# Low parts of weight blocks formed in one piece, and keys by three matmuls in the convolution stages

## The chip, the cores and the metric

The program runs on one core of one Trainium2 chip. The metric is the device time of one execution in microseconds (us). Engines are named as the profile names them: PE (TensorE, with PEld for its weight loads), DVE (VectorE), ACT (ScalarE), POOL (GpSimd), SP (SyncE, which issues the weight loads from memory).

## The reference

A decoder trunk of four layers works on 256 positions of width 1024, in fp32. Layers 0 and 3 mix positions with a gated causal convolution of 31 taps, layer 1 with a state-space scan, layer 2 with differential attention. Every layer then attends to 256 memory positions and ends in a gated feed-forward. Each sub-layer is added to its scaled input and normalized. What the change touches is the keys of the memory attention; every product of the kernel with a weight matrix uses the low parts.

```python
def memory_cross_attention(x, mem, w_q, w_kv, w_out):
    q = (x @ w_q).reshape(b, s, XA_HEADS, XA_HEAD_DIM) * (XA_HEAD_DIM ** -0.5)
    k, v = jnp.split(mem @ w_kv, 2, axis=-1)
    ...
    p = jax.nn.softmax(jnp.einsum('bshd,bmhd->bhsm', q, k), axis=-1)
    return jnp.einsum('bhsm,bmhd->bshd', p, v).reshape(b, s, D_MODEL) @ w_out

for i in range(DEPTH):          # 4 layers
    y = (conformer_conv, ssd_mixer, diff_attention)[i % 3](x, ...)
    x = post_norm(x, y, ...)
    x = post_norm(x, memory_cross_attention(x, mem, ...), ...)
    x = post_norm(x, swiglu(x, ...), ...)
```

## The kernel before, in words

**Products.** An fp32 product is made of matmuls in the faster type F32R. Every operand is split into a high part (rounded to that type) and a low part (what the rounding left). A product is then high by high, high by low and low by high; `mm3` writes these three matmuls (L199, L200, L201).

**Weights.** All weights pass through `_Weights` in blocks of 128 x 1024 elements, in an order that a dry run of the same program has written down (`plan`). `_load` issues a block's transfer on SP (L145) into one of four raw buffers, rounds it on ACT into the high part `wh` (L152), and subtracts on DVE for the low part `wl` (L155), in `LO_PARTS` pieces. `wh` and `wl` have seven buffers each (`RING`). A call of `get` hands out the next block and first sees to it that the three blocks after it (`AHEAD`) have been asked for.

**Memory projection.** `mem @ w_kv` does not depend on the layer's input. It is cut into eight units a layer (`kv_steps`): units 0 to 3 make 256 columns of the keys each, units 4 to 7 of the values. Units are called at fixed places, so that TensorE has work while another engine finishes a stage: in layer 0's convolution four units after the transform of the first half of the channels and three after the norm's code (`KV_CONV`), in layer 3's one and four; one after the feed-forward's first block and one after the feed-forward, for the next layer. So the convolution of layer 0 calls key units 0 to 3, and that of layer 3 key units 2 and 3.

**Keys.** A key unit runs `gemm_c_steps`. The memory's high and low parts lie side by side in one tile (`MT`, 512 columns), so one 512-column matmul (L277) multiplies the weights' high part with both; a 256-column matmul (L279) adds the low part of the weights times the high part of the memory, into the right half of the PSUM bank. Both weight blocks of the unit are asked for at the start. The two halves of 128 output columns use one bank each, out of the two of pool `psI`; `summed` evicts a half by an ACT copy of the bank's left half (L292) and a DVE add of its right half (L293), into `memK`.

**Values** use `mm3` with 256-column matmuls into a single bank of `psI`, block by block, and are split by ACT and DVE (L206, L208) into `memVh` and `memVl`.

**The convolution's tail.** After the depthwise transform, DVE and ACT normalize and gate the tile (DVE L586, L592, L595, ACT L594), TensorE transposes it (L598), and ACT and DVE split it (L206, L210) for the output product (L321, L322, L325).

**Norms.** `post_norm` is a chain of DVE steps (L365, L242, L243, L233, L372, L377) with a POOL step, then transposes (L219) and splits into `XT` (L206, L208), from which the next sub-layer starts.

**Order.** Pools, waits and the order of instructions on every engine are set when the program is built: a list scheduler with a cost model takes the next ready instruction by its place in the program, and `post_norm` is moved ahead by 400 places (`high_priority`). An engine then runs its instructions in that fixed order.

Of the kernel before, what the change touches and what calls it, by code (L numbers as in the profile page):

```python
# [60 lines left out]

RING = 7
RAW = 4
LO_PARTS = 2
AHEAD = 3
KV_CONV = ((4, 3), (1, 4))
KV_SSD = (0, 0, 0, 0, 0, 0, 0, 1, 2, 1)
# [42 lines left out]
class _Weights:  # L110
# [25 lines left out]
    def _load(self, q):  # L136
# [15 lines left out]
        nc.scalar.copy(out=wh, in_=raw)  # L152
        m = nk * n // LO_PARTS
        for a in range(0, nk * n, m):
# [9 lines left out]
class _Trunk:  # L164
# [257 lines left out]
    def kv_steps(self, layer):  # L422
        u = self.kv_next
        if u >= 8 * min(layer + 1, DEPTH):
            return
        self.kv_next += 1
        i, u = divmod(u, 8)
        nc = self.nc
        if u < 4:
            yield from self.gemm_c_steps(  # L430
                "xa_w_kv", i, ((u * 256, 256),), self.MT, self.summed(self.memK[:, 2 * u : 2 * u + 2, :])
            )
            return
        ps = self.bank("i", a=2)
        for b in range(2):
            wh, wl = self.W.get("xa_w_kv", i, 4 * b, 4, (u * 256, 256))
            for k in range(4):
                kk = 4 * b + k
                for m in range(T):
                    ms = slice(m * P, (m + 1) * P)  # L440
                    self.mm3(
                        ps[:, m, :], self.MTh[:, kk, ms], self.MTl[:, kk, ms], wh[:, k, :], wl[:, k, :],
                        kk == 0 and m == 0, kk == KT - 1 and m == 1,
                    )
            yield
        cs = slice((u - 4) * 256, (u - 3) * 256)
        self.split(ps, self.memVh[:, :, cs], self.memVl[:, :, cs])
# [911 lines left out]
    def run(self):  # L1359
        n = 0  # L1360
        ctx = ExitStack()
        pre, (loads, tables, late) = self.prepare(0, ctx, _FromRaw(self.raw))
        loads()
        self.setup()
        tables()
        pre["late"] = late
        for i in range(DEPTH):
            m, j = i % 3, i // 3
            (self.conv, self.ssd, self.diff)[m](i, j, pre)
            ctx.close()  # L1370
            if i == 0:
                self.rope()
            n += 1
            if n == self.n_sub:
                break
            self.xattn(i)
            n += 1
            if n == self.n_sub:
                break
            hooks, tmp = {}, ExitStack()  # L1380
            if i < DEPTH - 1:
                made = {}
                pre, steps = self.prepare(i + 1, ctx, _Late(made))
                made["pool"] = tmp.enter_context(self.stage_pool(f"tmp{i + 1}", 1))
                hooks = {3 + 2 * k: [step] for k, step in enumerate(steps)}
            self.ff(i, i < DEPTH - 1, hooks)
            tmp.close()
            n += 1
            if n == self.n_sub:
                break  # L1390
            self.kv_unit(i + 1)
        ctx.close()
        if n != N_SUB:
            for t in range(T):
                self.nc.sync.dma_start(out=self.out[0][t * P : (t + 1) * P, :], in_=self.x[t])
# [37 lines left out]
```

## Time and profile before

| | |
|---|---|
| median of 3 runs | 1755.23 us (1751.21 to 1758.06) |
| the profiled execution | 1751.45 us |
| its span, first to last instruction | 1749.7 us |
| PE busy, matmuls | 1705.1 us, 9692 of them |
| DVE busy | 1324.2 us, 2514 instructions |
| ACT busy | 912.6 us, 1442 instructions |
| POOL busy | 57.1 us, 72 instructions |

The profile is of one execution; times in it count from the first instruction. A matmul's record reaches beyond the start of the next one, since they are pipelined, so the rate of a stream is read from start to start. In a timeline the bracket at the end of a row gives the engine's idle time before that instruction and what ended it.

### The profile page before, as it was taken

The numbers are of one execution on the slowest core, as the hardware profiler recorded it, in microseconds if no ns is written. First come the engines' busy times: TensorE is split into PE (matmuls) and PEld (weight loads), VectorE is DVE, ScalarE is ACT, GpSimd is POOL, SyncE is SP. The second block draws the span as 40 slices with busy tenths as digits, with TensorE's granted clock in tenths as the row PEclk, the third lists the DMA queues.
The fourth block names the chain that finished last, engine by engine and source line by source line (L and its number), as shares of the span: only waits on it lengthen the run. The fifth ranks groups of instructions, "written<-read, shape, count | busy, mean of one in ns | idle before, by whom it ended". The sixth has DMA issues, their size and how long they took to land.

```text
span 1749.7 us, 26246 instructions
## 1 busy us (share of the span) xinstructions
PE 1705.1 (97%) x9692; PEld 1466.5 (84%) x9692; DVE 1324.2 (76%) x2514; ACT 912.6 (52%) x1442; POOL 57.1 (3%) x72
## 2 busy tenths in 40 slices
PE   7999999999999999999999999999999998999998
PEld 4788888888999998888888888988788787878886
DVE  5889786668998878786668677876666897876666
ACT  3545555554665655455554565645454544645552
POOL 0000000000011010000000000000000000000000
PEclk9999999999999999999999999999999999999999
DMA  7647466665755645476665543656566635646662
GB/s 232 205 126 231 137 209 188 184 190 172 222 166 171 187 145 186 121 220 190 192 192 179 183 133 109 193 167 199 171 187 191 216 109 181 192 159 193 191 190 75
DMA packets 234088, 309.86 MB, mean 177 GB/s; under 512 B 14104, under 2 KB 196774, under 8 KB 233960
## 3 DMA queue, kind: packets, MB, share of 16 engines
q1 hardware_dynamic: 233832, 307.90, 57.2%
q8 instruction: 76, 1.25, 0.3%
q14 instruction: 52, 0.43, 0.1%
q10 hardware_dynamic: 128, 0.29, 0.0%
HBM read 307.07 MB, written 1.08 MB: 176 GB/s over the span
## 4 chain that ended last, share of the span: by engine, by line
PE 81%; DVE 5%; DMA 2%; ACT 1%; issue 1%; POOL 0%; SPq 0%; DVEq 0%; ACTq 0%; POOLq 0%
PE psi L277 20%; PE psi L279 10%; PE pso L321 6%; PE pso L322 6%; PE pso L325 6%; PE psi L199 5%; PE psi L200 5%; PE psi L201 5%; PE pso L199 4%; PE pso L201 4%; PE pso L200 4%; DVE wl L155 1%; PE psm L219 1%; DVE st L242 1%; DMA raw<-in_xa_w_q 1%
## 5 line engine op out<-in xcount | busy, mean ns | idle before, releaser
L155 DVE TENSOR_TENSOR wl<-raw,wh 128x512 fp32r<-128x512 f32 x1074 | 708.2, 687 | 288.4 <-ACT wh L152 280.4
L152 ACT CAST wh<-raw 128x1024 fp32r<-128x1024 f32 x537 | 561.9, 1052 | 467.4 <-issue 125.4
L277 PE MATMUL psi<-XT,wh 128*128 128x512 f32 x1408 | 387.1, 396 | 0.0
L277 PEld LDWEIGHTS psi<-XT,wh 128*128 128x128 f32 x1408 | 243.6, 189 | 36.7 <-issue 2.4
L279 PEld LDWEIGHTS psi<-XT,wl 128*128 128x128 f32 x1408 | 216.5, 189 | 29.9
L279 PE MATMUL psi<-XT,wl 128*128 128x256 f32 x1408 | 224.4, 281 | 0.0
L321 PE MATMUL pso<-wh,ch 128*128 128x512 f32 x448 | 176.4, 394 | 0.5 <-ACT ch L206 0.5
L322 PE MATMUL pso<-wl,ch 128*128 128x512 f32 x448 | 175.4, 392 | 0.0
L325 PE MATMUL pso<-wh,cl 128*128 128x512 f32 x448 | 138.6, 391 | 0.0
L199 PE MATMUL psi<-XT,wh 128*128 128x256 f32 x384 | 111.3, 290 | 0.0
L201 PE MATMUL psi<-XT,wl 128*128 128x256 f32 x384 | 108.7, 283 | 0.0
L200 PE MATMUL psi<-XT,wh 128*128 128x256 f32 x384 | 108.6, 283 | 0.0
L325 PEld LDWEIGHTS pso<-wh,cl 128*128 128x128 f32 x448 | 84.0, 188 | 17.9
L321 PEld LDWEIGHTS pso<-wh,ch 128*128 128x128 f32 x448 | 84.1, 188 | 16.6 <-ACT ch L206 0.9
L322 PEld LDWEIGHTS pso<-wl,ch 128*128 128x128 f32 x448 | 84.2, 188 | 15.8
L199 PE MATMUL pso<-wh,XT 128*128 128x512 f32 x224 | 89.2, 399 | 0.1
L201 PE MATMUL pso<-wh,XT 128*128 128x512 f32 x224 | 88.4, 395 | 0.3 <-DVE XT L208 0.3
L200 PE MATMUL pso<-wl,XT 128*128 128x512 f32 x224 | 87.8, 392 | 0.0
L234 POOL TENSOR_TENSOR rs<-rv,mhalf 128x1 f32<-128x1 f32 (+2 forms) x40 | 37.0, 926 | 1320.8 <-DVE rv L233 1308.5
L199 PE MATMUL pso<-wh,ch 128*128 128x512 f32 x192 | 75.9, 396 | 0.0
L201 PE MATMUL pso<-wh,cl 128*128 128x512 f32 x192 | 75.1, 392 | 0.0
L199 PE MATMUL psi<-wh,MT 128*128 128x256 f32 x256 | 74.6, 291 | 0.4 <-DVE memVl L208 0.4
(324 smaller groups left out, 2941.8 us busy)
## 6 DMA issues: line engine op xcount, KB each, us to landing
raw<-in_ff_w_in SPq DMA_DIRECT2D x160, 512.0 KB, 4.6
raw<-in_ff_w_out SPq DMA_DIRECT2D x88, 512.0 KB, 4.0
raw<-in_xa_w_kv SPq DMA_DIRECT2D x64, 512.0 KB, 4.5
raw<-in_cv_w_in SPq DMA_DIRECT2D x64, 256.0 KB, 4.2
raw<-in_xa_w_q SPq DMA_DIRECT2D x32, 512.0 KB, 4.3
raw<-in_xa_w_out SPq DMA_DIRECT2D x32, 512.0 KB, 4.7
raw<-in_mb_w_in SPq DMA_DIRECT2D x32, 512.0 KB, 3.9
raw<-in_da_w_qkv SPq DMA_DIRECT2D x24, 512.0 KB, 4.6
```

Of the source, the lines that this page charges most:

```text
L152: nc.scalar.copy(out=wh, in_=raw)
L155: nc.vector.tensor_tensor(out=wl[:, a : a + m], in0=raw[:, a : a + m], in1=wh[:, a : a + m].bitcast(F32), op=ALU.subtract)
L199: mm(out, ah, bh, start=start, stop=False)
L200: mm(out, ah, bl, start=False, stop=False)
L201: mm(out, al, bh, start=False, stop=stop)
L219: nc.tensor.transpose(ps[:, i, :], nat[:, (4 * j + i) * P : (4 * j + i + 1) * P], self.ident)
L234: nc.gpsimd.tensor_tensor(out=r, in0=v, in1=self.mhalf[:, :cols], op=ALU.pow)
L277: mm(ps, wh[:, k, js], X[:, 4 * b + k, :], start=b == 0 and k == 0, stop=False)
L279: mm(ps[:, S : 2 * S], wl[:, k, js], X[:, 4 * b + k, 0:S], start=False, stop=b == 1 and k == 3)
L321: mm(acc[t][c], hh[:, ts], wh[:, 0, cs], start=first, stop=False)
L322: mm(acc[t][c], hh[:, ts], wl[:, 0, cs], start=False, stop=False)
L325: mm(acc[t][c], hl[:, ts], wh[:, 0, cs], start=False, stop=last)
```

## The change

`LO_PARTS` goes from 2 to 1: the low part of a block is one DVE instruction of 1024 columns. In the convolution stages (`in_conv`) a key unit runs `gemm_b_steps`, the form that the state-space layer uses already: three 256-column matmuls (`mm3`) for each pair of 128 rows and 128 columns, block by block, all into one PSUM bank, which a single ACT copy of 512 columns then evicts. Key units called elsewhere stay as they are.

```diff
--- before.py
+++ after.py
@@ -61,7 +61,7 @@
 
 RING = 7
 RAW = 4
-LO_PARTS = 2
+LO_PARTS = 1
 AHEAD = 3
 KV_CONV = ((4, 3), (1, 4))
 KV_SSD = (0, 0, 0, 0, 0, 0, 0, 1, 2, 1)
@@ -426,12 +426,16 @@
         self.kv_next += 1
         i, u = divmod(u, 8)
         nc = self.nc
-        if u < 4:
+        if u < 4 and not self.in_conv:
             yield from self.gemm_c_steps(
                 "xa_w_kv", i, ((u * 256, 256),), self.MT, self.summed(self.memK[:, 2 * u : 2 * u + 2, :])
             )
             return
         ps = self.bank("i", a=2)
+        if u < 4:
+            yield from self.gemm_b_steps(ps, "xa_w_kv", i, ((u * 256, 256),), self.MTh, self.MTl)
+            nc.scalar.copy(out=self.memK[:, 2 * u : 2 * u + 2, :], in_=ps)
+            return
         for b in range(2):
             wh, wl = self.W.get("xa_w_kv", i, 4 * b, 4, (u * 256, 256))
             for k in range(4):
@@ -1366,7 +1370,9 @@
         pre["late"] = late
         for i in range(DEPTH):
             m, j = i % 3, i // 3
+            self.in_conv = m == 0
             (self.conv, self.ssd, self.diff)[m](i, j, pre)
+            self.in_conv = False
             ctx.close()
             if i == 0:
                 self.rope()
```

## Rows read from the trace of the kernel before

**Rows 1.** The page: engine table, then the chain by engine and by line.
```profile
PE 1705.1 (97%) x9692; PEld 1466.5 (84%) x9692; DVE 1324.2 (76%) x2514; ACT 912.6 (52%) x1442; POOL 57.1 (3%) x72
...
PE 81%; DVE 5%; DMA 2%; ACT 1%; issue 1%; POOL 0%; SPq 0%; DVEq 0%; ACTq 0%; POOLq 0%
PE psi L277 20%; PE psi L279 10%; PE pso L321 6%; PE pso L322 6%; PE pso L325 6%; PE psi L199 5%; PE psi L200 5%; PE psi L201 5%; PE pso L199 4%; PE pso L201 4%; PE pso L200 4%; DVE wl L155 1%; PE psm L219 1%; DVE st L242 1%; DMA raw<-in_xa_w_q 1%
```

**Rows 2.** VectorE by line and form: count, busy us, mean ns, idle before.
```profile
L155 DVE TENSOR_TENSOR wl<-raw,wh 128x512 fp32r<-128x512 f32 x1074 | 708.2, 687 | 288.4 <-ACT wh L152 280.4 <-PE psm L965 1.0
...
L293 DVE TENSOR_TENSOR memK<-memK,psi 128x256 f32<-128x256 f32 x32 | 13.1, 418 | 2.0 <-ACT memK L292 1.7
...
L565 DVE SCALAR_TENSOR_TENSOR x<-x,raw 128x1024 f32<-128x1024 f32 x4 | 4.8, 1218 | 0.0
```

**Rows 3.** TensorE timeline of layer 3's convolution tail: start, us, instruction, idle before.
```profile
1436.06 0.28 PE L199 MATMUL psi<-wh,MT 128*128 128x256 f32 x1
1436.18 0.28 PE L200 MATMUL psi<-wl,MT 128*128 128x256 f32 x1
...
1443.28 0.28 PE L201 MATMUL psi<-wh,MT 128*128 128x256 f32 x1
1444.45 0.63 PE L598 MATMUL psm<-ident,cv_u 128*128 128x128 f32 x4 [0.89 <-DVE rv L233]
...
1450.00 1.09 PE L598 MATMUL psm<-ident,cv_u 128*128 128x128 f32 x4 [3.28 <-DVE cv_u L595]
1450.74 0.56 PE L199 MATMUL psi<-wh,MT 128*128 128x256 f32 x1
```

**Rows 4.** TensorE timeline of layer 0, first key unit.
```profile
61.67 0.63 PE L279 MATMUL psi<-MT,wl 128*128 128x256 f32 x4
64.99 0.43 PE L199 MATMUL psm<-ch,cv_dft0h 128*82 128x512 f32 x1 [2.69 <-DVE cvp L541]
```

**Rows 5.** VectorE timeline between the steps of a norm, layer 0.
```profile
220.25 0.68 DVE L155 TENSOR_TENSOR wl<-raw,wh 128x512 fp32r<-128x512 f32 x1
...
225.15 0.64 DVE L155 TENSOR_TENSOR wl<-raw,wh 128x512 fp32r<-128x512 f32 x1
...
228.41 1.29 DVE L155 TENSOR_TENSOR wl<-raw,wh 128x512 fp32r<-128x512 f32 x2
```

**Rows 6.** TensorE timeline in the same norm.
```profile
229.24 0.36 PE L279 MATMUL psi<-MT,wl 128*128 128x256 f32 x1
```

**Rows 7.** TensorE timeline of a key unit, layer 0.
```profile
72.01 1.08 PE L277 MATMUL psi<-MT,wh 128*128 128x512 f32 x4
72.92 0.64 PE L279 MATMUL psi<-MT,wl 128*128 128x256 f32 x4
73.40 1.09 PE L277 MATMUL psi<-MT,wh 128*128 128x512 f32 x4
```

**Rows 8.** TensorE timeline after the tail of layer 3.
```profile
1455.41 0.41 PE L201 MATMUL psi<-wh,MT 128*128 128x256 f32 x1
1455.62 0.39 PE L199 MATMUL psi<-wh,MT 128*128 128x256 f32 x1
```

**Rows 9.** ScalarE timeline in the tail of layer 3.
```profile
1436.75 0.36 ACT L292 COPY memK<-psi 128x256 f32<-128x256 f32 x1
```

**Rows 10.** VectorE timeline in the tail of layer 3.
```profile
1436.18 0.64 DVE L155 TENSOR_TENSOR wl<-raw,wh 128x512 fp32r<-128x512 f32 x1
...
1449.77 0.42 DVE L293 TENSOR_TENSOR memK<-memK,psi 128x256 f32<-128x256 f32 x1
1450.10 0.69 DVE L155 TENSOR_TENSOR wl<-raw,wh 128x512 fp32r<-128x512 f32 x1
```

**Rows 11.** Busy time by stretch: us and instructions of each engine, granted clock, DMA.
```profile
60.00:128.00 68.00, 64.87 (x380) 55.73 (x378) 57.97 (x104) 33.53 (x49) 1.11 (x2) 1.00 0.44 135
1429.00:1450.00 21.00, 16.36 (x102) 13.84 (x101) 20.06 (x39) 10.38 (x18) 1.10 (x2) 0.98 0.15 51
1449.00:1456.00 7.00, 6.00 (x29) 5.96 (x30) 7.00 (x15) 4.06 (x8) 0.00 (x0) 0.51 0.56 182
```

## Prediction

> **What bounds the kernel now.** I read the page's engine table and chain first [rows 1]: TensorE is busy for 1705.1 of 1749.7 us and holds 81% of the chain, VectorE is busy for 76% and holds 5%, with the low-part line L155 at 1%. So the matmul stream sets the time; a change that takes work off VectorE pays only where TensorE stands still for VectorE. All such standing still together is at most 1749.7 - 1705.1 = 44.6 us. Next I read VectorE by line and form [rows 2], for the size of what is edited, and then the TensorE timeline, looking for idle times in brackets; two of the larger ones lie in convolution stages: 3.28 us near 1450 and 2.69 us near 62 [rows 3, 4].
>
> **Low parts, one instruction instead of two.** There are 1074 / 2 = 537 blocks. A half of 512 columns takes 0.687 us [rows 2]; the 1024-column line L565 (other operation, same shape and element type, both tensors in SBUF) takes 1.218 us. Summed by durations a block would save 2 x 0.687 - 1.218 = 0.156 us. But VectorE's instructions overlap at their ends: 1074 x 0.687 is 738 us while the line is busy for 708.2, and two halves in a row take 1.29 us from the first's start to the second's end (last row of [rows 5]), 0.084 us less than two durations; so each frees the engine about 0.084 us before its end, a pair holds it for 1.29 - 0.084 = 1.206 us and a whole for 1.218 - 0.084 = 1.134. I take 0.07 us a block, 537 x 0.07 = 38 us of VectorE's 1324. [...]
>
> On TensorE's time this is worth 0 in my sum, because the matmuls already run over it. Bounds: if every L155 on the chain (1% of 1749.7, 17 us) shrinks by 0.07 in 1.20, -1.0 us. The other end is loss: a whole cannot be interrupted. Between the steps of a norm, VectorE now slips single halves in: four from 220.25 to 225.15 [rows 5]. If each of the four becomes a whole, the norm is 4 x 0.53 = 2.1 us later (0.53 being 1.218 - 0.687). Eleven norms feed a following sub-layer: 44 x 0.53 = 23 us. The work that hides this is the memory projection, of which pieces lie between the transposes of the norm (L279 on MT in [rows 6]); a unit holds 5.6 us of it and little is used up there. I take 0, nearer to the hidden end, since TensorE's row there has no idle time in front of it. The first use of a low part may also wait up to 0.53 us longer, but blocks are asked for three ahead, which is some 9 us of matmuls at 3.3 us a block (1749.7 / 537); in the steady stretches that stays hidden.
>
> **Keys: matmuls.** Six units change: four in layer 0, two in layer 3 (u = 2 and 3, since units 24 and 25 run in the feed-forward before). Old: per four k, four 512-column matmuls in 0.91 us and four of 256 in 0.48 [rows 7]; a unit has four such groups, 4 x 1.39 = 5.56 us. New: 48 matmuls of 256 columns, which the value units already run at 0.12 us from start to start (first two rows of [rows 3]): 5.76 us. Cost 6 x 0.20 = +1.2 us, taken in full as TensorE is the bound. [...]
>
> **Keys: eviction and bank.** A unit now has two ScalarE copies and two VectorE adds of 0.418 us [rows 2]; afterwards one ScalarE copy of 512 columns, no VectorE work. Copies: less than the two of 0.36 us that they replace [rows 9], hidden by ScalarE's idle half: 0. Adds: about 0.33 us of the engine each, 12 x 0.33 = 4 us of VectorE. What counts is which bank comes free when. In layer 3's tail ScalarE copies the second key half at 1436.75 [rows 9], but the add that frees its bank runs at 1449.77 [rows 10], behind the convolution's norm, on a VectorE that is busy for 20.06 of 21 us [rows 11]. There are two such banks and the other holds the value unit that ran from 1436.06 to 1443.28 (48 matmuls) [rows 3]. So TensorE had no bank for the next value unit: it idled 0.89 and 3.28 us and started that unit at 1450.74 [rows 3], right after the add. With the change the bank is free at about 1437.4. What is late next is the low part of that unit's weights: its halves run at 1436.18 and 1450.10 [rows 10], the first block only. As one instruction begun at 1436.18 the whole block is done at 1437.4, unless it is put behind the norm. Then TensorE has 24 matmuls x 0.12 = 2.9 us to run in the gap; the second block of 24 waits. Gain 2.9 us (bounds 0, and 4.2 for both gaps).
>
> **The clock.** [...] An idle of 2.69 us at 64.99 left the clock alone (the 60-to-128 stretch shows 1.00 [rows 11]), so with the gap broken by 2.9 us of matmuls I expect no fall: -2.5 us (bounds 0 and -2.5).
>
> **Layer 0.** At 61.67 the first key unit has run its first 4 + 4 matmuls, then TensorE waits 2.69 us for the bank of the transform [rows 4]. In the old order a unit's half needs both weight blocks; in the new one block gives 24 matmuls, 2.88 us instead of 1.39. Gain 1.5 us (bounds 0, 2.7). The second block is asked for up to 2.9 us later than now; the order of loads is the same, and three blocks ahead cover it: 0, up to 2.9 once if not.
>
> **Sum.** +1.2 - 2.9 - 2.5 - 1.5 + 0 = -5.7 us against the profiled execution's 1751.45 us (span 1749.7 and 1.75 around it): 1745.8. That execution lies 3.8 us under the median of the runs shown, 1755.23; on the median's scale I predict 1749.5, 0.3% down. About 0.5%, 8.8 us, is what a measurement of this kernel can tell from no change.
>
> **Rivals.**
> *VectorE remains the wall.* In the tail the whole low part is put behind the norm, so the free bank has nothing to run. For it: VectorE has 0.94 us of slack in 21 [rows 11], and the second half now runs only at 1450.10 [rows 10]. Against: the first half did get in at 1436.18. The tail's -5.4 is gone: +1.2 - 1.5, 1754.9.
> *More is given back.* Both tail gaps vanish (4.2), the clock holds (2.5), layer 0's gap goes entirely (2.7) and the chain's low parts shrink (1.0): +1.2 - 10.4 = -9.2, 1746.0. For it: every idle here names VectorE. Against: the second block's low part has to come from the same full engine.
> *Whole low parts hold up the norms; slower.* 0.53 us at each of 44 places [rows 5], if the projection pieces no longer cover them. It makes the kernel slower than before from 11 uncovered places on (5.7 / 0.53), slower by over 0.5% from 28 on; at 28, 1764. For it: VectorE's steps of a norm follow each other with hardly any idle. Against: no idle TensorE there now.
> [...]
>
> **Chances.** Forecast 0.43 (own range 1747 to 1753), wall 0.27, more given back 0.15, norms 0.13, loads 0.02. Faster by over 0.5%: most of the third case and the forecast's lower edge, 0.17; slower: the last two, 0.14 after some of the norm case falls short; within: 0.69. Range 1742 to 1762: it takes in the first three with some 3 us of spread between medians at either end, and leaves out the last two.
>
> **What would show it.** L155 with 537 instructions of about 1.22 us; VectorE's busy time down by some 40 us; L293 on memK 20 times instead of 32. Right: in layer 3's tail value matmuls between 1443 and 1450, no idle over 2 us there and the granted clock at 1.00. Wrong: the same 3 us of idle before L598 and the low clock behind it, or new idle of half a microsecond before XT's first matmuls at the norms. What would upset the whole is that the order written for every engine changes with 537 instructions fewer, and a new gap arises somewhere that this trace doesn't show.

## The result, and the profile after

The changed kernel takes 1745.11 us (median of 19 runs, 1740.33 to 1753.83), the kernel before beside it 1755.23 (19 runs): ratio over all runs 0.9949, 95% interval 0.9937 to 0.9960 (the two medians alone give 0.9942). That is 0.51% faster by the ratio, just over the bound that the prediction set for telling a change. 1745.1 lies in the range, 2 us under the forecast's own range and 4.4 under its 1749.5. The profiled execution took 1743.85 us, span 1742.1 against 1749.7. Line numbers shift by a few between the kernels: L602 below is L598 of the kernel before.

The page's engine table, which answers to [rows 1]:

```profile
PE 1702.5 (98%) x9788; PEld 1470.3 (84%) x9788; DVE 1283.5 (74%) x1965; ACT 907.8 (52%) x1436; POOL 67.8 (4%) x72
```

VectorE by line and form, which answers to [rows 2]:

```profile
L155 DVE TENSOR_TENSOR wl<-raw,wh 128x1024 fp32r<-128x1024 f32 x537 | 654.1, 1221 | 286.3 <-ACT wh L152 281.5 <-DMA raw<-in_xa_w_kv 1.8 <-PE psm L969 1.7
...
L293 DVE TENSOR_TENSOR memK<-memK,psi 128x256 f32<-128x256 f32 x20 | 8.2, 408 | 0.9 <-ACT memK L292 0.6
```

VectorE has 40.7 us less to do, and TensorE's busy time is 2.6 us shorter although it has 96 matmuls more. Layer 3's convolution tail, TensorE's timeline and then the windows; these answer to [rows 3, 11]:

```profile
1443.95 0.60 PE L602 MATMUL psm<-ident,cv_u 128*128 128x128 f32 x4
1444.30 0.36 PE L200 MATMUL psi<-wl,MT 128*128 128x256 f32 x1
...
1445.70 0.63 PE L602 MATMUL psm<-ident,cv_u 128*128 128x128 f32 x4
1446.08 0.36 PE L199 MATMUL psi<-wh,MT 128*128 128x256 f32 x1
```

```profile
1428.00:1449.00 21.00, 21.00 (x159) 19.85 (x158) 19.93 (x36) 11.37 (x19) 1.10 (x2) 1.00 0.32 101
```

No row there has a bracket: 0.89, 0.47 and 3.28 us of idle are gone, value matmuls run on both sides of the transposes, and the granted clock is 1.00. Layer 0's gap stayed as long, which answers to [rows 4]:

```profile
63.64 0.28 PE L201 MATMUL psi<-MT,wl 128*128 128x256 f32 x1
63.76 0.28 PE L199 MATMUL psi<-MT,wh 128*128 128x256 f32 x1
66.74 0.43 PE L199 MATMUL psm<-ch,cv_dft0h 128*82 128x512 f32 x1 [2.70 <-DVE cvp L545]
```

One place that the prediction did not look at also changed: the start of layer 3's convolution. In the kernel before, TensorE's timeline and VectorE's in the same stretch:

```profile
1364.59 1.29 PE L219 MATMUL psm<-ident,x 128*128 128x128 f32 x8
1368.59 0.47 PE L199 MATMUL psi<-wh,XT 128*128 128x512 f32 x1 [2.71 <-DVE memK L293]
```

```profile
1361.75 0.65 DVE L155 TENSOR_TENSOR wl<-raw,wh 128x512 fp32r<-128x512 f32 x1
...
1365.02 1.30 DVE L155 TENSOR_TENSOR wl<-raw,wh 128x512 fp32r<-128x512 f32 x2
1366.22 1.29 DVE L208 TENSOR_TENSOR XT<-psm,XT 128x512 fp32r<-128x512 f32 x2
1367.41 0.69 DVE L155 TENSOR_TENSOR wl<-raw,wh 128x512 fp32r<-128x512 f32 x1
1368.01 0.76 DVE L293 TENSOR_TENSOR memK<-memK,psi 128x256 f32<-128x256 f32 x2
```

Afterwards, in VectorE's timeline, the same two adds stand among the norm's steps and right behind them, both ahead of the last low part and of the second half's XT splits; TensorE is busy for all of the 12 us from 1360 on:

```profile
1361.44 0.36 DVE L293 TENSOR_TENSOR memK<-memK,psi 128x256 f32<-128x256 f32 x1
...
1364.43 0.41 DVE L293 TENSOR_TENSOR memK<-memK,psi 128x256 f32<-128x256 f32 x1
1364.76 1.22 DVE L155 TENSOR_TENSOR wl<-raw,wh 128x1024 fp32r<-128x1024 f32 x1
```

This key unit is unit 25, which runs with the old key matmuls in both kernels. So here the low parts moved the adds. That raised the question which of the two edits the gain belongs to.

### The profile page after: what moved, and what is told of

Its sections match the earlier page's. It is cut to its first block, busy times and chain, and to the rows that moved or that the text cites. A ratio compares the mean times of both kernels' runs of the same rounds, so it can differ in the third digit from the quotient of the medians.

```text
span 1742.1 us, 25792 instructions
## 1 busy us (share of the span) xinstructions
PE 1702.5 (98%) x9788; PEld 1470.3 (84%) x9788; DVE 1283.5 (74%) x1965; ACT 907.8 (52%) x1436; POOL 67.8 (4%) x72
## 5 line engine op out<-in xcount | busy, mean ns | idle before, releaser
L155 DVE TENSOR_TENSOR wl<-raw,wh 128x1024 fp32r<-128x1024 f32 x537 | 654.1, 1221 | 286.3 <-ACT wh L152 281.5
L277 PEld LDWEIGHTS psi<-XT,wh 128*128 128x128 f32 x1408 | 242.9, 189 | 37.8 <-PE psm L201 2.6
L322 PE MATMUL pso<-wl,ch 128*128 128x512 f32 x448 | 175.2, 391 | 0.0
L325 PE MATMUL pso<-wh,cl 128*128 128x512 f32 x448 | 139.8, 391 | 0.0
L234 POOL TENSOR_TENSOR rs<-rv,mhalf 128x1 f32<-128x1 f32 (+2 forms) x40 | 48.5, 1212 | 1337.0 <-DVE rv L233 1324.2
L200 PE MATMUL pso<-wl,ch 128*128 128x512 f32 x192 | 75.0, 391 | 0.0
L199 PEld LDWEIGHTS psi<-XT,wh 128*128 128x128 f32 x384 | 73.6, 192 | 0.7 <-issue 0.3
```

The costliest lines, as they stand in the source:

```text
L155: nc.vector.tensor_tensor(out=wl[:, a : a + m], in0=raw[:, a : a + m], in1=wh[:, a : a + m].bitcast(F32), op=ALU.subtract)
L199: mm(out, ah, bh, start=start, stop=False)
L200: mm(out, ah, bl, start=False, stop=False)
L234: nc.gpsimd.tensor_tensor(out=r, in0=v, in1=self.mhalf[:, :cols], op=ALU.pow)
L277: mm(ps, wh[:, k, js], X[:, 4 * b + k, :], start=b == 0 and k == 0, stop=False)
L322: mm(acc[t][c], hh[:, ts], wl[:, 0, cs], start=False, stop=False)
```

## The experiments

**Which part.** The theory of the prediction's sum, that ScalarE frees the keys' bank in time, against its rival, that whole low parts do it.

*Low parts whole, keys as before.*

```diff
-LO_PARTS = 2
+LO_PARTS = 1
```

> Whole low parts alone, key units as before. Theory of the bank (the gain of the change comes from layer 3's convolution tail, where a key half holds its bank until an add on a full VectorE): the tail keeps a gap of over 2 us before L598 and a fall of the granted clock behind it, the whole kernel changes by -2 to +2 us. Rival of the low parts (shorter VectorE work gives the gain by itself): -7 to -10 us, gap gone.

Measured: 1743.65 us beside 1752.97, ratio 0.9950 (0.9937 to 0.9962), span 1741.9. This is the whole gain without any new key unit. VectorE's busy time is 1287.2 us by the page, 37.0 under [rows 1]. Its timeline in the tail has the second half's add at 1435.60, right behind the first statistics of the convolution's norm (L581), where [rows 10] have it at 1449.77 behind the norm:

```profile
1434.89 0.67 DVE L543 TENSOR_TENSOR cv_yre<-cvp,cv_yre 81x512 f32<-81x512 f32 x1
1435.48 0.20 DVE L581 BATCH_NORM_AGGREGATE mv<-st 128x2 f32<-128x12 f32 x1
1435.60 0.36 DVE L293 TENSOR_TENSOR memK<-memK,psi 128x256 f32<-128x256 f32 x1
1435.88 0.68 DVE L544 TENSOR_TENSOR cvp<-psm,cv_H 81x512 f32<-81x512 f32 x1
```

*Keys new, low parts in halves.*

```diff
+            self.in_conv = m == 0
...
-        if u < 4:
+        if u < 4 and not self.in_conv:
...
+        if u < 4:
+            yield from self.gemm_b_steps(ps, "xa_w_kv", i, ((u * 256, 256),), self.MTh, self.MTl)
+            nc.scalar.copy(out=self.memK[:, 2 * u : 2 * u + 2, :], in_=ps)
+            return
```

> Key units of the convolution stages as in the changed kernel, low parts in two halves as before. Theory of the bank: the tail of layer 3 has a bank early, -5 to -9 us, with at most 2 us of idle left there where a second block's low part is late. Rival of the low parts: +1 us (48 matmuls for 32 in six units), gap as before. Third theory, both parts needed (the bank comes free but the low part is still behind the norm): 0 to -2 us here and in the run with whole low parts alone.

Measured: 1751.91 us, ratio 0.9996 (0.9984 to 1.0009): no change. Yet the tail's idle is gone here too. TensorE is busy for all of the tail at clock 1.00 (windows), while its timeline keeps the start's idle and shows a new one at the next norm:

```profile
1431.00:1452.00 21.00, 21.00 (x150) 19.06 (x149) 20.32 (x38) 10.91 (x17) 1.10 (x2) 1.00 0.29 94
```

```profile
1372.12 0.77 PE L199 MATMUL psi<-wh,XT 128*128 128x512 f32 x1 [2.70 <-DVE memK L293]
...
1482.45 0.39 PE L201 MATMUL pso<-wh,cl 128*128 128x512 f32 x1
1485.24 1.29 PE L219 MATMUL psm<-ident,x 128*128 128x128 f32 x8 [2.41 <-DVE x L377]
```

ScalarE's and VectorE's timelines ahead of that norm:

```profile
1477.66 1.05 ACT L152 CAST wh<-raw 128x1024 fp32r<-128x1024 f32 x1 [1.62 <-DMA raw<-in_xa_w_q]
```

```profile
1478.74 1.29 DVE L155 TENSOR_TENSOR wl<-raw,wh 128x512 fp32r<-128x512 f32 x2 [1.37 <-ACT wh L152]
1479.95 0.68 DVE L365 SCALAR_TENSOR_TENSOR x<-x,pso 128x512 f32<-128x512 f32 x1
1480.67 0.69 DVE L242 BATCH_NORM_STATS2 st<-x 128x6 f32<-128x512 f32 x1
1481.28 0.67 DVE L365 SCALAR_TENSOR_TENSOR x<-x,pso 128x512 f32<-128x512 f32 x1
```

Read from the bottom: the norm's first step L365 is written behind the low part of a block whose load came late, so that the cast waited 1.62 us for the DMA and the low part 1.37 us for the cast. TensorE, now ahead of the loads, runs out of matmuls. Part of the idle went from the tail to the norm behind it: up to that norm's first transpose this profile is 3.4 us ahead of the kernel before (129.34 against 132.75 us from the stage's first L365), and of these the medians show 1.1 (1752.97 - 1751.91), not told from nothing. Here the second L365 (1481.28) waits for nothing of TensorE's, it is only late in VectorE's order, while in the kernel before it waited 1.30 us for TensorE (VectorE's timeline):

```profile
1481.17 0.69 DVE L365 SCALAR_TENSOR_TENSOR x<-x,pso 128x512 f32<-128x512 f32 x1 [1.30 <-PE pso L201]
```

*The changed kernel, with VectorE copying the keys out.*

```diff
-            nc.scalar.copy(out=self.memK[:, 2 * u : 2 * u + 2, :], in_=ps)
+            nc.vector.tensor_copy(out=self.memK[:, 2 * u : 2 * u + 2, :], in_=ps)
```

> The changed kernel with the key units' copy out of the bank on VectorE instead of ScalarE: same matmuls, same low parts, the bank again waits for VectorE. Theory of the bank: the gap in layer 3's tail comes back, 3 us or more, and the clock falls behind it, so +5 to +8 us against the changed kernel, -4 to 0 against the kernel before. Rival of the low parts, and that of the matmul form (one bank per unit instead of one per half is what helps): within 2 us of the changed kernel, -7 to -10 against before.

Measured: 1746.35 us, ratio 0.9964 (0.9952 to 0.9977). The tail has no idle although VectorE frees the bank, at 1439.84:

```profile
1439.84 0.63 DVE L437 COPY memK<-psi 128x512 f32<-128x512 f32 x1
```

So it is not the engine that matters but the place in its order.

*The changed kernel, with new key units in layer 3 only.*

```diff
-            self.in_conv = m == 0
+            self.in_conv = i == 3
```

> The changed kernel with the new key units in layer 3's convolution alone; layer 0 keeps the old ones. Theory of the bank: the four units of layer 0 gave nothing (its gap near 62 us stayed), and cost 0.2 us each on TensorE, so -9 to -11 us against before, 0 to 1 better than the changed kernel. Rival, layer 0 has a share: -5 to -7.

Measured: 1744.06 us, ratio 0.9954 (0.9940 to 0.9968). With or without layer 0's new units the time is the same.

**Volume or order.** After these runs two theories of the whole low parts were left: VectorE has some 40 us less to do (volume), or the written order of VectorE changes so that the key adds, which free TensorE's banks, come earlier in layer 3 (order).

*Halves as before, the adds put early.*

```diff
-            self.nc.scalar.copy(out=out[:, j, :], in_=main)
-            self.nc.vector.tensor_tensor(out=out[:, j, :], in0=out[:, j, :], in1=rest, op=ALU.add)
+            with self.tc.high_priority() if early else ExitStack():
+                self.nc.scalar.copy(out=out[:, j, :], in_=main)
+                self.nc.vector.tensor_tensor(out=out[:, j, :], in0=out[:, j, :], in1=rest, op=ALU.add)
...
+                "xa_w_kv", i, ((u * 256, 256),), self.MT, self.summed(self.memK[:, 2 * u : 2 * u + 2, :], early=True)
```

> Halves as before, old keys; only the two adds of each key unit (L293 on memK) and the copies ahead of them are put into VectorE's order as early as they can run: in layer 3's tail the second half's add stands some 11 instructions earlier, at the convolution's start the two adds no longer stand behind both blocks' halves. Order theory (the gain came from adds that free a bank in time, 2.7 us at the start of layer 3's convolution, 4.2 us of gaps and 2.5 us of low clock in its tail): ratio 0.995, some 1744 to 1747 us beside a kernel before of 1753, the convolution stage of layer 3 some 118 us long instead of 126. Volume theory (40 us less VectorE work is what counts): VectorE's work is the same, so 1752 to 1754, ratio 0.9995.

Measured: 1744.7 us beside 1752.96, ratio 0.9957 (0.9941 to 0.9972), as order said. VectorE's work is unchanged (page), its timeline has the tail's second add at 1437.12, where [rows 10] have 1449.77, and TensorE is busy through the tail (windows). The edit names only the adds and the copies ahead of them; the scheduler then placed other work anew too, and in and just behind layer 3's convolution some 25 of the 198 other VectorE instructions, low parts among them, stand elsewhere in the order:

```profile
PE 1701.9 (98%) x9692; PEld 1463.8 (84%) x9692; DVE 1322.5 (76%) x2514; ACT 912.3 (52%) x1442; POOL 56.5 (3%) x72
```

```profile
1437.12 0.42 DVE L294 TENSOR_TENSOR memK<-memK,psi 128x256 f32<-128x256 f32 x1 [0.19 <-ACT memK L293]
```

```profile
1437.00:1457.00 20.00, 20.00 (x160) 19.29 (x159) 19.31 (x38) 11.85 (x22) 1.47 (x2) 1.00 0.36 122
```

*Two pieces of 960 and 64 columns.*

```diff
-        for a in range(0, nk * n, m):
+        for a, e in ((0, 960), (960, 1024)):
...
-                out=wl[:, a : a + m], in0=raw[:, a : a + m], in1=wh[:, a : a + m].bitcast(F32), op=ALU.subtract
+                out=wl[:, a:e], in0=raw[:, a:e], in1=wh[:, a:e].bitcast(F32), op=ALU.subtract
```

> A block's low part in two instructions of 960 and 64 columns instead of 512 and 512: the same number of instructions and columns, so the same VectorE time as before (some 1320 us busy), old keys. Volume theory: as before, ratio 1.000. Order theory: it depends on where the key adds fall in the written order: at the start of layer 3's convolution they stand together behind the blocks as before (2.7 us idle stays), in the tail the second add stands in the middle of the norm, some 3 us earlier than before, so that about 1 us of 4.2 idle and perhaps the clock's 2.5 us come back: ratio 0.998 to 1.000, 1749 to 1753 us. If what counts is the length of the longer piece alone: ratio 0.995.

Measured: 1757.66 us, ratio 1.0027 (1.0013 to 1.0040), outside what either theory gave. VectorE by line and form:

```profile
L154 DVE TENSOR_TENSOR wl<-raw,wh 128x960 fp32r<-128x960 f32 x537 | 620.3, 1155 | 286.7 <-ACT wh L152 274.7 <-PE psm L964 3.2 <-PE psi L276 2.6
L154 DVE TENSOR_TENSOR wl<-raw,wh 128x64 fp32r<-128x64 f32 x537 | 117.2, 218 | 0.0
```

Nearly the same VectorE time (1319.7 us by the page, 4.5 less) and a longer piece make it slower. A long piece is therefore no gain in itself. The order moved here too, and against the kernel: by the page TensorE stands still for 51.2 us (1755.3 - 1704.1) instead of 44.6. In layer 3's convolution it stands still for 3.8 us less (table below); so some 10 us more of idle lie in the other stages, spread over many gaps (one execution each).

*Whole low parts only from layer 2's feed-forward to the end of layer 3's convolution, and the complement.*

```diff
-        m = nk * n // LO_PARTS
+        m = nk * n // (1 if self.whole else LO_PARTS)
...
+            self.W.whole = i == 3
             (self.conv, self.ssd, self.diff)[m](i, j, pre)
+            self.W.whole = False
...
+            self.W.whole = i == 2
             self.ff(i, i < DEPTH - 1, hooks)
```

That is the stretch; the complement has `i != 3` and `i != 2` in these places, and `True` for `False`.

> Whole low parts only for blocks that are asked for from the feed-forward of layer 2 to the end of layer 3's convolution, halves everywhere else, old keys. Order theory: the key adds there stand as with whole low parts throughout, so nearly the whole gain: ratio 0.995 to 0.996, 1745 to 1747 us, layer 3's convolution some 119 us. Volume theory: these are about a fifth of the blocks, so a fifth of the gain: ratio 0.999, 1751 us.

> The complement: halves for the blocks from layer 2's feed-forward to the end of layer 3's convolution, whole low parts everywhere else, old keys. Order theory: layer 3's convolution keeps its idle at the start (2.7 us) and in the tail (4.2 us and the low clock): ratio 0.999 to 1.000, 1751 to 1753 us. Volume theory: four fifths of the gain, ratio 0.996, 1746 us.

Measured: 1742.15 us, ratio 0.9931 (0.9916 to 0.9947) for the stretch, and 1753.29 us, ratio 1.0000 (0.9991 to 1.0009) for all the rest. The complement saves most of VectorE's time (page) and keeps layer 3's idle (TensorE's timeline):

```profile
PE 1704.0 (97%) x9692; PEld 1466.5 (84%) x9692; DVE 1295.3 (74%) x2081; ACT 910.0 (52%) x1442; POOL 67.3 (4%) x72
```

```profile
1367.56 0.47 PE L201 MATMUL psi<-wh,XT 128*128 128x512 f32 x1 [2.71 <-DVE memK L295]
...
1448.96 1.09 PE L600 MATMUL psm<-ident,cv_u 128*128 128x128 f32 x4 [3.28 <-DVE cv_u L597]
```

28.9 us less VectorE work (1324.2 - 1295.3) for nothing; a saving of 7.9 us (its page has 1316.3) in the right stretch for at least as much as the whole change. The volume theory falls.

**Start and tail apart.**

*Only the start's two adds early (unit 25), in the kernel before and in the one with the new key units alone.* `summed` has its `early` as above; the call is:

```diff
+                "xa_w_kv", i, ((u * 256, 256),), self.MT, self.summed(self.memK[:, 2 * u : 2 * u + 2, :], early=(i, u) == (3, 1))
```

> As the kernel before, but only the two adds of the one key unit that runs while layer 3's convolution starts are put early in VectorE's order. Order theory, the two places priced apart: the 2.7 us idle at the start goes, the tail keeps its 4.2 us idle and the low clock, so about a third of what all early adds gave: ratio 0.998, some 1750 us, the stage some 123 us instead of 126. If the start alone carried the gain: ratio 0.996; if the tail alone did: 1.000.

> The new key units alone (which left the time unchanged, 0.9996) with the two adds at the start of layer 3's convolution put early as well. If the keys gained nothing because the start's idle was left: 0.9955 to 0.997, 1746 to 1748 us, the stage under 121 us. If the 1.5 us of added matmuls and new idle in other stages eat the tail's gain: 0.998, 1749 us or more.

Measured: 1752.05 us beside 1753.88, ratio 0.9989 (0.9975 to 1.0002), and 1753.53 us, ratio 0.9998 (0.9984 to 1.0012). 1.8 us and 0.4 us, neither told from nothing; the second expectation's first case is wrong. TensorE's timeline of the former shows why:

```profile
1405.02 0.43 PE L199 MATMUL psm<-ch,cv_dft1h 128*82 128x512 f32 x1 [2.17 <-DVE cvp L542]
...
1452.30 0.63 PE L599 MATMUL psm<-ident,cv_u 128*128 128x128 f32 x4 [3.28 <-DVE cv_u L596]
```

The start's idle is gone and 2.17 us stand 35 us later, before the second half's transforms. VectorE's timeline there:

```profile
1402.02 0.69 DVE L155 TENSOR_TENSOR wl<-raw,wh 128x512 fp32r<-128x512 f32 x1 [0.28 <-ACT wh L152]
1402.63 0.68 DVE L519 TENSOR_TENSOR cva<-psi,cvb 128x512 f32<-128x512 f32 x1
1403.23 0.68 DVE L541 TENSOR_TENSOR cvp<-psm,cv_H 81x512 f32<-81x512 f32 x1
```

Again the steps that TensorE waits for stand behind a low part that waits for its cast. The kernel with new keys has the same there (2.27 us) and 3.02 us at the norm behind the tail.

*The partial whole low parts with all key adds early.*

```diff
+            self.W.whole = i == 3
...
+            self.W.whole = i == 2
...
+                "xa_w_kv", i, ((u * 256, 256),), self.MT, self.summed(self.memK[:, 2 * u : 2 * u + 2, :], early=True)
```

> Whole low parts only from layer 2's feed-forward to the end of layer 3's convolution, and all key adds early. Order theory: the adds of layer 3 stood early already and TensorE shows no idle for the others, so as with the partial whole parts alone: ratio 0.993, 1741 to 1744 us. Rival: early adds help in the other layers too: 0.991 or less.

Measured: 1741.22 us, ratio 0.9926 (0.9899 to 0.9953): as without the early adds, within the intervals. Either is a little under the changed kernel, by less than the intervals tell.

*The kernel before, profiled once more.*

> The kernel before, profiled once more. What its order sets repeats: in layer 3 idle of 2.7 us at the start, 0.9 and 3.3 us in the tail and the low clock behind them. If the low clock of 6.8 us near 1248 comes from the order as well, it is there again; if it comes and goes between runs, it may be missing, and the feed-forward of layer 2 is then some 199 to 201 us long instead of 203.

Measured: one time of 1758.47 us. TensorE's timeline repeats the tail's gaps to 0.01 us, and the windows show the low clock of layer 2's feed-forward again:

```profile
1457.36 0.91 PE L598 MATMUL psm<-ident,cv_u 128*128 128x128 f32 x4 [3.28 <-DVE cv_u L595]
```

```profile
1251.00:1260.00 9.00, 9.00 (x24) 5.46 (x24) 3.36 (x7) 0.60 (x2) 0.00 (x0) 0.62 0.46 158
```

The clock behind layer 3's gaps does not repeat. Behind the start's 2.70 us it is low for nearly 7 us here and was not low at all in the first profile (windows, this profile and then the first):

```profile
1372.30:1379.00 6.70, 5.87 (x14) 4.65 (x15) 4.80 (x10) 2.09 (x2) 0.00 (x0) 0.50 0.95 316
```

```profile
1372.00:1379.00 7.00, 7.00 (x33) 5.79 (x32) 5.05 (x9) 4.67 (x6) 0.00 (x0) 1.00 0.92 287
```

**Layer 3's convolution in all profiles.** TensorE's idle (brackets of its timeline over 0.4 us) at the start, before the transforms or the gate, in the tail, and at the norm behind; low clock is the time for which the granted clock is 0.5 of full, with the gap in or behind which it fell; the stage is counted from the first L365 of the norm ahead to that of the norm behind, from VectorE's timeline. Us throughout.

| kernel | start | transforms | tail | norm behind | low clock | stage | ratio |
|---|---|---|---|---|---|---|---|
| before | 2.71 | 0 | 0.89 + 0.47 + 3.28 | 0 | 6.8 (tail) | 126.1 | 1 |
| before, again | 2.70 | 0 | 0.90 + 0.47 + 3.28 | 0 | 6.8 (start) + 3.4 (tail) | 127.9 | - |
| whole except here | 2.71 | 0 | 0.90 + 0.47 + 3.28 | 0 | 3.4 (tail) | 124.7 | 1.0000 |
| start's adds early | 0 | 2.17 | 0.90 + 0.47 + 3.28 + 0.55 | 0 | 3.4 (transforms) + 3.4 (tail) | 126.3 | 0.9989 |
| 960 + 64 | 0.45 + 2.24 | 0 | 0.84 | 0 | 3.4 (start) | 122.5 | 1.0027 |
| new keys only | 2.70 | 0 | 0 | 2.41 | 3.4 (start) | 124.1 | 0.9996 |
| new keys, start's adds early | 0 | 2.27 | 0 | 3.02 | 3.4 (transforms) + 3.4 (norm) | 124.1 | 0.9998 |
| changed, VectorE copies the keys | 0 | 1.22 | 0 | 0 | 0 | 117.5 | 0.9964 |
| changed, layer 3's keys only | 0 | 2.23 | 0 | 0 | 3.4 (transforms) | 119.6 | 0.9954 |
| all adds early, halves | 0 | 1.91 | 0 | 0.80 | 0 | 119.4 | 0.9957 |
| whole only | 0 | 1.66 | 0 | 0.53 | 0 | 119.1 | 0.9950 |
| changed kernel | 0 | 1.77 | 0 | 0 | 0 | 117.6 | 0.9949 |
| whole here only | 0 | 1.87 | 0 | 0 | 3.4 (transforms) | 120.4 | 0.9931 |
| whole here, adds early | 0 | 0 | 0 | 0 | 0 | 117.2 | 0.9926 |

Each profile is one execution: the first three have the same order in layer 3, and their stage is 124.7 to 127.9 us long. The kernels that gain over 0.3% are those with a stage of 117 to 121 us: no idle in the tail and under 1 us at the norm behind it. The tail's idle follows the instruction that frees the second bank of the last key unit (line memK<-psi, by the timelines, counted from the stage's first L365): at 97.4 to 100.2 us in the profiles with 3.28 us, at 93.7 in 960 + 64 with 0.84, at 81.5 to 87.2 in all with none, whichever engine runs it.

## Why the prediction was right, and where it was not

**Whole low parts at 0: the step that failed.** The sizes were right: 1.221 us an instruction against 1.218, and 37.0 us of VectorE for whole parts alone against 38. In the rows under "Layer 0" below the whole from 63.21 takes 1.23 us and the next instruction starts 1.14 us after its start, where the prediction had 1.134. What failed was "On TensorE's time this is worth 0 in my sum", with -1.0 as its best end. Whole parts alone measured 9.3 us (1752.97 - 1743.65). The time lies in the stated range by luck: the -5.7 was to come from the key units, which alone give nothing that can be told, while the term put at 0 gives by itself what the whole change gives, 10.1 us between the medians (8.9 by the ratio), within the intervals. The prediction priced what a shorter instruction saves and what it delays; it did not price that another length puts everything else on VectorE in another place. The upset named in its last sentence did happen, in the kernel's favour.

**Keys, bank and tail: the place was right, the owner was not.** The tail's gaps and the low clock behind them are where time was won: the stage is 8.4 us shorter (126.06 - 117.63), of which 0.89 + 0.47 + 3.28 are the tail's gaps, some 2.5 to 3 the clock of this profile before (an estimate: 5.8 to 6.8 us with 256-column matmuls every 0.21 us [rows 8] instead of every 0.12 [rows 3]) and 2.71 - 1.77 the start less what came back before the transforms; the forecast had 2.9 + 2.5, its bounds 4.2 + 2.5. The bank was what TensorE waited for there: freeing it early by ScalarE's copy (new keys alone) and freeing it early by moved adds both remove all three gaps, and the kernels that leave the tail's adds late keep them. But the new key units are not needed for it, and alone they give 0 instead of -5.7: 2.41 us of idle come back at the next norm, and the start keeps its 2.70, in that profile with 3.4 us of low clock behind it. What else they lose is not located. "What is late next" was answered with one low part, the value unit's own; it should have been followed to the next norm.

**The keys' matmuls, +1.2.** 18 steps from 61.62 to 63.76 in the changed kernel's first key unit are 0.119 us each, so 48 are 5.7 us as priced. Each of these matmuls has a weight load of its own, 0.19 us long in TensorE's load timeline, and the loads too start every 0.12 us, beside the matmuls: nothing is seen there of a cost for the added loads, to which the chances give 0.02. The 1.2 us cannot be told from nothing in the times.

**The clock, -2.5.** Right that the fall goes with the tail's gap: 1.00 through the tail, where [rows 11] have 0.51. No run shows the 2.5 us as such. What the profile before shows in its place is a granted clock of 0.50 for 6.8 us; TensorE is at work in the last 5.8 of them, from 1450.00 on, with a 256-column matmul every 0.21 us [rows 8] instead of every 0.12 [rows 3], from which 5.8 x (1 - 0.12 / 0.21) = 2.5 us is an estimate. That size is of one execution: in the three other profiles with the same gap the clock was low for 3.4 us, which halves the term. And the premise that 2.69 us of idle leave the clock alone holds of that profile and not of every one: in the second profile of the same kernel the clock is 0.50 from 64.9 to 68.3, at layer 0's 2.70 us, and again behind the start's 2.70. The prediction had one profile to read.

**Layer 0, -1.5.** Wrong: 2.70 us stay, released by the transform's L545. The gate step L522 stands behind two low parts that wait for casts. VectorE's timeline:

```profile
61.75 1.22 DVE L155 TENSOR_TENSOR wl<-raw,wh 128x1024 fp32r<-128x1024 f32 x1 [1.46 <-ACT wh L152]
63.21 1.23 DVE L155 TENSOR_TENSOR wl<-raw,wh 128x1024 fp32r<-128x1024 f32 x1 [0.23 <-ACT wh L152]
64.35 0.68 DVE L522 TENSOR_TENSOR cva<-psi,cvb 128x512 f32<-128x512 f32 x1
```

TensorE did get its 19 matmuls of the first block in front of the gap, and then waited as long as before (2.70 us against 2.69): more matmuls ahead of a wait help only if the wait's end does not move with them.

**The rivals.** "VectorE remains the wall" describes the keys alone, 30 us further on than it was put. "More is given back" has the nearest time (1746.0), by both tail gaps and the clock, but layer 0's 2.7 did not come. The norms that whole parts were to hold up did not show: neither whole parts alone nor whole parts in a part of the program made the kernel slower. The time came near it for a reason that neither sum had.

**What stays open.** In layer 2's feed-forward the clock is low for some 7 us near 1250 in some profiles (windows, before and then after):

```profile
1240.00:1262.00 22.00, 22.00 (x86) 15.04 (x86) 13.31 (x22) 7.67 (x12) 0.00 (x0) 0.84 0.46 140
```

```profile
1240.00:1262.00 22.00, 22.00 (x102) 16.00 (x101) 14.68 (x20) 10.13 (x15) 0.00 (x0) 1.00 0.53 163
```

0.16 of 22 us is 3.5 us, and the stage is 4.0 us shorter by the same count as above (202.83 to 198.83). Two of the six profiles with whole parts there show the fall as well, and one of the eight with pieces shows none, so the change is not shown to have removed it. Other stages are longer by some 5 us together (7.6 in the span is less than 8.4 + 4.0); which of that is the order's and which one execution's own was not settled. "Whole here only" is 10.8 us faster by the medians, but its stage only 5.7 us shorter; the rest is not located. Nor was it followed why the scheduler puts the adds earlier when the low parts are whole.

## What to carry to other kernels

VectorE works here in written order, and a filler that waits for a load delays all that stands behind it (1.37 us ahead of the norm's L365 with the new keys alone, 1.46 and 0.23 us ahead of the gate step L522 in the changed kernel); so before pricing a change of a filler's length by its duration, list which short instructions free a bank or start a norm and where they will stand. Put those few by hand ahead of the filler, and look at what the scheduler moves along with them: here 32 adds of 0.4 us, moved and not shortened, gave what 537 merged instructions did, within the intervals. A gap that closes can let the matmuls run into the loads (2.41 us of idle at the next norm with the new keys alone): follow the stream to the next norm before counting the gap as won.

## What was not expected of the hardware

Layer 3's gaps repeat to 0.01 us from run to run and between kernels that share the order there (3.28 us in four profiles); others in the same order do not (0.68 and 1.92 us at the norm behind layer 0's convolution). The clock behind a gap does not repeat: behind the same 3.28 us it was low for 6.8 us once and for 3.4 three times, and behind the start's 2.7 us low for 6.8 us in one profile of the kernel before and not at all in the other. And VectorE's load as such told nothing of the time: 29 us less in one kernel left it at 1.0000, nearly the same load in uneven pieces raised it by 0.27%.
